# High and low weight parts of the first mixer: sixteen tiles by rounding and adding transfers instead of ScalarE and VectorE, and a moved product

## Chip, cores and metric

The kernel runs on one core of a Trainium2 chip. The metric is the device time of one execution in microseconds (us). The three runs of the kernel before lie between 2079.13 and 2080.56 us, with a median of 2079.3 us. The engines are PE (TensorE; PEld is its weight load), DVE (VectorE), ACT (ScalarE), POOL (GpSimd) and SP (SyncE, which issues transfers).

## What is computed

Two layers of a diffusion backbone over 1024 latent tokens of 1024 channels, with 256 context tokens. Layer 0 mixes tokens by a bidirectional linear recurrence (RG-LRU), layer 1 by a gated short convolution; each is followed by a gated feed-forward part with a convolution. The change lies in the first mixer, cut here to its core:

```python
def rglru_coeffs(u, w_r, b_r, w_i, b_i, lam):
    ub = u.reshape(bsz, n, LRU_HEADS, LRU_BLOCK)            # 4 heads of 256 channels
    r = sigmoid(einsum('bnhi,hij->bnhj', ub, w_r) + b_r)
    i = sigmoid(einsum('bnhi,hij->bnhj', ub, w_i) + b_i)
    log_a = LRU_C * r * log_sigmoid(lam)
    return exp(log_a), sqrt(-expm1(2.0 * log_a)) * (i * u)

def rglru_mixer(hl, hc, ...):                               # hl latent, hc context
    ul = seq_conv(hl @ w_x, conv_w, conv_b, CONV_A_PAD)
    uc = seq_conv(hc @ w_x, conv_w, conv_b, CONV_A_PAD)
    hl_f = scan of the latent, forward, from the last state of the context
    hl_b = the same, backward
    return (gelu(hl @ w_gate) * (hl_f + hl_b)) @ w_out
```

All inputs and the output are float32.

## The kernel before, in words

**Products in two parts.** A float32 operand is split into a high part, rounded to the matmul type fp32r, and a low part, the rest. A product of two split operands takes three matmuls, high by high, high by low and low by high (`mm`). The split of a weight tile (`split`, called in `weight_item`) is an ACT instruction that writes `wh` from the loaded tile `raw`, and a DVE subtraction that writes `wl` from `raw` and `wh`. Channels lie on the 128 partitions in eight chunks, tokens along the free dimension.

**Units and slots.** The program is a list of units, each with the weight tiles that it needs. The first mixer's list is the string `ORDER`:

- `g`*m* is the gate product of channel chunk *m* and `x`*m* the latent product with `w_x`: 48 matmuls of 512 columns each, one 128x1024 weight tile (`wg`, `wx`);
- `ctx` holds the eight context products xc0 to xc7, 24 matmuls of 256 columns each;
- `us`*m* splits the convolved inputs of chunks *m* and *m*+1 into `uh` and `ul`;
- `r`*m* is a recurrence block: 48 matmuls of 512 columns and 24 of 256 with two `wri` tiles, one for each direction, then tanh, exp, sqrt on ACT and products and scans on DVE in seven `mx` tiles. Both blocks of a head, r0 and r1, r2 and r3 and so on, use the same two `wri` tiles;
- `e`*n* and `d`*n* are *n* dot products of DVE over `ada` rows, which later layers need. Those of `e` go through `mx` tiles, those of `d` through the single tile `acct`.

Weight tiles live in six half-width slots, which hold three tiles of 1024 columns at a time. A slot is free when its last matmul has read it. `raw` tiles come on SP's queue into three buffers, ahead of the split. The small `cs` tile holds, before the recurrence, a weighted sum of weight rows and the squares of the context's norm; `xc` is the context itself.

**Order.** Instructions are recorded, and a planner (`Plan.flush`) sets the order on each engine by costs (`cost`), delays between engines (`lag`) and due times. PE's order is the program's own. Each engine works strictly in its order, and so does each queue of transfers. The out-projection `o` follows r7; its first unit multiplies three weight tiles with all eight output chunks of the mixer, chunk by chunk.

Of the kernel before, what the change touches and what calls it, by code (L numbers as in the profile page):

```python
# [8 lines left out]
F32 = mybir.dt.float32  # L9
F32R = mybir.dt.float32r  # L10
AF = mybir.ActivationFunctionType
ALU = mybir.AluOpType
# [5 lines left out]
HALF = 512  # L18
# [12 lines left out]
for _n, _w in _VEC:  # L31
# [10 lines left out]
DOTS = (0, 0, 0, 1, 1, 2, 2, 2)  # L42


ORDER = ("g2 shift g3 norm g4 g5 ctx mx us0 e6 x4 r0 d3 x5 d2 r1 d2 us2 x6 d1 r2 d1 x7 d1 r3 d1 us4 d1 r4 d1 g6 r5 "
         "us6 g7 r6 r7")

TABLE = {AF.Silu: (AF.Silu, AF.Tanh), AF.Gelu_apprx_tanh: (AF.Gelu_apprx_tanh, AF.Tanh), AF.Sqrt: (AF.Sqrt,),
# [3 lines left out]
class Plan:  # L52
# [48 lines left out]
    @staticmethod  # L101
    def cost(engine, op, a, k):

        if engine == "sync":
            return 4 * int(np.prod(a[0].shape)) / 360e3
        n = max(int(np.prod(v.shape[1:])) for v in list(a) + list(k.values()) if isinstance(v, bass.AP))
        if engine == "tensor":
            n = a[2].shape[-1]
            return max(n, 128) / 2400 * (4 if a[2].dtype == F32 else 1)
        if engine == "scalar":  # L110
            return 0.09 + n * 0.85e-3 + (0.09 if "accum_out" in k else 0)
        if engine == "gpsimd":
            return 0.15 + n * (2.1e-3 if op == "tensor_tensor" else 0.84e-3)
        return 0.07 + n * (6.25e-3 if op == "reciprocal" else 1.05e-3)

    @staticmethod
    def lag(a, b):

        return 0.0 if a == b else 0.95 if a == "sync" else 1.9 if b == "sync" else 0.2

    def flush(self):
        ops, first, last = self.ops, self.todo, len(self.ops)
# [61 lines left out]
def hybrid_kernel(ctx: ExitStack, tc: tile.TileContext, out, xs, cs, c, cc, ada, vecs,  # L184
                  ident, w0, wx, wg, wo, wri, wbi, wbo, wup, wdn):
    nc = Plan(tc)
    V, S, T, G = nc.vector, nc.scalar, nc.tensor, nc.gpsimd
# [37 lines left out]
    def sub(o, a, b, eng=None):  # L225
        (eng or V).tensor_tensor(out=o, in0=a, in1=b, op=ALU.subtract)

    def act(o, i, f, bias=0.0, scale=1.0):
        S.activation(o, i, f, bias=bias, scale=scale)

    def split(hi, lo, src, eng=None):
        if eng is None:
            act(hi, src, AF.Identity)
        else:
            eng.tensor_scalar(out=hi, in0=src, scalar1=1.0, scalar2=0.0, op0=ALU.mult, op1=ALU.add)
        sub(lo, src, hi.bitcast(F32))
# [17 lines left out]
    x = xp.tile([P, KD, SEQ], F32, tag="x", name="x")  # L254
# [21 lines left out]
    weight_hi = [None]  # L276
# [23 lines left out]
    def wsrc(key):  # L300
        kind = key[0]
        if kind in ("x", "xc"):
            return wx[key[1]]
        if kind == "g":
            return wg[key[1]]
        if kind == "o":
            return wo[key[1]]
        if kind == "ri":
            return wri[key[1]]
        if kind == "bo":  # L310
            return wbo[key[1]]
        return wdn[key[1], key[2], :, 2 * D:]
# [9 lines left out]
    def flat(t, i, n):  # L322
        return t[:, i:i + n].rearrange("p a b -> p (a b)") if n > 1 else t[:, i]

    def weight_item(key):
        src = wsrc(key)
        n = src.shape[-1]

        def prep(sl, raws):
            hi, lo = flat(sl[0][0], sl[0][2], len(sl))[:, :n], flat(sl[0][1], sl[0][2], len(sl))[:, :n]  # L330
            split(hi, lo, raws[0].tile[:, :n], weight_hi[0])
            return hi, lo
        return Item(key, [Raw(src)], -(-n // HALF), prep)

    def block_items(name, src1, src2, again):

# [32 lines left out]
    def run_units(nside):  # L369
# [3 lines left out]
        for i, (_, keys) in enumerate(units):  # L373
            for k in keys:
                if k not in seen:
                    seen[k] = i
                    stream.append(items[k] if k in items else weight_item(k))
                    for _ in range(nside(k)):
                        if side:
                            src, dst, bt, eng = side.pop(0)  # L380
                            stream.append(Item(None, [Raw(src)], 0, lambda sl, raws, dst=dst, bt=bt, eng=eng:
                                               dot(dst, raws[0].tile, bt, eng)))
                last[k] = i
# [487 lines left out]
    shifts = start()  # L871
    for o in ORDER.split():
        if o[0] == "g":
# [571 lines left out]
```

## Time and profile before

| What | Value |
|---|---|
| median of 3 runs | 2079.3 us |
| the profiled execution, its own time | 2082.59 us |
| its span, first to last instruction | 2080.8 us |
| PE busy | 2036.8 us (98%) |
| DVE busy | 1764.5 us (85%) |
| ACT busy | 1049.3 us (50%) |
| POOL busy | 0.2 us |
| mean granted TensorE clock | 0.993 of full speed |

The 1.8 us by which the profiled execution's time exceeds its span lie around the first and last instruction. Shares over the whole span hide the stage of interest: the first mixer lies between 100 and 400 us. A timeline row gives the start, the duration, the engine, the program line, the operation with out<-in and the shape; brackets at its end give the idle time before it and what ended that. All instructions carry line 165, that of the planner's issue, so tiles tell them apart. Consecutive instructions of DVE and ACT overlap slightly, so what one takes on its engine is read from start to start.

### The profile page before, as it was taken

To read this page: it belongs to the slowest core of one execution; us is meant where nothing else is said; L and a number is where in the kernel's file an instruction comes from. 1 tells how busy PE (TensorE), PEld (TensorE's weight loads), DVE (VectorE), ACT (ScalarE), POOL (GpSimd) and SP (SyncE) were. 2 spreads that over 40 slices of the span, in tenths; PEclk is the share of its full clock that TensorE was granted. 3 is DMA by queue.
4 is the path that set the end of the run, shared out by engine and by line. 5 is a ranking of instruction groups with operands and counts; after the bars stand their busy time and mean duration, and the time that the engine had idled before them with its cause. 6 is when DMAs were issued, how large, how long until landed. Compare 5 with 4: busy or idle time off the path is not lost.

```text
span 2080.8 us, 25029 instructions
## 1 busy us (share of the span) xinstructions
PE 2036.8 (98%) x9218; PEld 1681.5 (81%) x9218; DVE 1764.5 (85%) x2624; ACT 1049.3 (50%) x1574; POOL 0.2 (0%) x4
## 2 busy tenths in 40 slices
PE   8899989999999999999999999999999999999998
PEld 6688877787888888878888788888888888878888
DVE  7998999979888888798769988858988887688867
ACT  6366878546544444535255433435644444464345
POOL 0000000000000000000000000000000000000000
PEclk9999999999999999999999999999999999999999
DMA  7544222551334455565361345652243443474345
GB/s 298 185 169 162 71 81 84 193 167 48 126 132 157 156 174 173 174 199 162 95 194 66 114 164 197 231 192 75 83 136 128 142 137 108 137 236 142 111 140 164
DMA packets 103418, 307.05 MB, mean 148 GB/s; under 512 B 10368, under 2 KB 14720, under 8 KB 103168
## 3 DMA queue, kind: packets, MB, share of 16 engines
q1 hardware_dynamic: 103296, 305.46, 44.6%
q8 instruction: 72, 1.18, 0.2%
q14 instruction: 50, 0.41, 0.1%
HBM read 248.80 MB, written 56.62 MB: 147 GB/s over the span
## 4 chain that ended last, share of the span: by engine, by line
PE 84%; DVE 9%; ACT 4%; DMA 2%; issue 1%; SPq 0%; DVEq 0%; ACTq 0%
PE banks L165 84%; ACT mx L165 2%; DVE x L165 2%; DVE mx L165 2%; DVE u L165 2%; DVE bl L165 2%; DMA x<-in_xs 1%; DVE wl L165 1%; DMA s<-bd 1%; ACT L165 1%; ACT bh L165 1%; DMA raw<-in_wg 0%; DVE uc L165 0%; DVE ul L165 0%; DVE acct L165 0%
## 5 line engine op out<-in xcount | busy, mean ns | idle before, releaser
L165 PE MATMUL banks<-bl,wh 128*128 128x512 f32 (+1 forms) x2720 | 1052.2, 387 | 11.0 <-DVE bl L165 10.9
L165 PE MATMUL banks<-bh,wh 128*128 128x512 f32 (+1 forms) x2720 | 1054.3, 388 | 3.2 <-ACT wh L165 1.6
L165 PE MATMUL banks<-bh,wl 128*128 128x512 f32 (+1 forms) x2720 | 1051.0, 386 | 2.6 <-DVE wl L165 2.5
L165 PEld LDWEIGHTS banks<-bl,wh 128*128 128x128 f32 x2720 | 511.6, 188 | 124.7 <-DVE bl L165 21.6
L165 PEld LDWEIGHTS banks<-bh,wh 128*128 128x128 f32 x2720 | 511.8, 188 | 109.0 <-ACT wh L165 2.0
L165 PEld LDWEIGHTS banks<-bh,wl 128*128 128x128 f32 x2720 | 511.6, 188 | 108.1 <-DVE wl L165 7.3
L165 ACT ACTIVATE wh<-raw 128x512 fp32r<-128x512 f32 (+2 forms) x386 | 275.6, 717 | 475.0 <-PE banks L165 394.7
L165 DVE TENSOR_TENSOR wl<-raw,wh 128x512 fp32r<-128x512 f32 (+2 forms) x386 | 303.2, 794 | 60.4 <-ACT wh L165 56.9
L165 DVE SCALAR_TENSOR_TENSOR x<-banks,mod,x 128x512 f32<-128x512 f32 (+1 forms) x184 | 132.6, 726 | 93.3 <-PE banks L165 92.3
L165 ACT ACTIVATE s<-banks 128x512 f32<-128x512 f32 x174 | 103.8, 596 | 195.0 <-PE banks L165 191.8
L165 ACT ACTIVATE wh<-s 128x512 fp32r<-128x512 f32 x216 | 135.5, 628 | 110.4 <-DVE s L165 63.7
L165 DVE TENSOR_TENSOR wl<-s,wh 128x512 fp32r<-128x512 f32 x216 | 148.5, 688 | 38.6 <-ACT wh L165 34.9
L165 DVE TENSOR_TENSOR s<-s,banks 128x512 f32<-128x512 f32 x158 | 107.8, 683 | 37.4 <-PE banks L165 36.9
L165 DVE SCALAR_TENSOR_TENSOR x<-s,vec,x 128x504 f32<-128x504 f32 x132 | 96.4, 740 | 10.2 <-ACT x L165 9.0
L165 DVE SCALAR_TENSOR_TENSOR acct<-acct,cb 128x1024 f32<-128x1024 f32 x69 | 84.1, 1218 | 4.5 <-DMA acct<-in_ada 4.5
L165 PE MATMUL banks<-uh,wh 128*128 128x512 f32 (+1 forms) x192 | 70.8, 369 | 8.1 <-ACT mx L165 7.0
L165 PE MATMUL banks<-ul,wh 128*128 128x512 f32 (+1 forms) x192 | 70.5, 367 | 3.1 <-DVE ul L165 3.1
L165 PE MATMUL banks<-uh,wl 128*128 128x512 f32 (+1 forms) x192 | 70.2, 366 | 0.0
L165 ACT ACTIVATE bh<-s 128x512 fp32r<-128x512 f32 x88 | 51.5, 624 | 35.3 <-DMA s<-bd 34.0
L165 ACT ACTIVATE bh<-x,cols 128x512 fp32r<-128x512 f32 x64 | 45.1, 721 | 42.1 <-DVE cols L165 27.3
L165 DVE TENSOR_TENSOR x<-x,s 128x512 f32<-128x512 f32 x90 | 61.0, 686 | 0.8
L165 DVE TENSOR_TENSOR bl<-s,bh 128x512 fp32r<-128x512 f32 x88 | 57.2, 684 | 5.0 <-ACT bh L165 5.0
(154 smaller groups left out, 1702.0 us busy)
## 6 DMA issues: line engine op xcount, KB each, us to landing
raw<-in_wup SPq DMA_DIRECT2D x92, 512.0 KB, 3.6
acct<-in_ada SPq DMA_DIRECT2D x69, 512.0 KB, 3.5
bd<-x SPq DMA_DIRECT2D x48, 512.0 KB, 3.2
s<-bd SPq DMA_DIRECT2D x44, 512.0 KB, 4.5
raw<-in_wdn SPq DMA_DIRECT2D x32, 512.0 KB, 4.4
raw<-in_wdn SPq DMA_DIRECT2D x40, 384.0 KB, 3.4
raw<-in_wbi SPq DMA_DIRECT2D x26, 512.0 KB, 4.1
u<-in_ada SPq DMA_DIRECT2D x24, 512.0 KB, 4.6
```

Source lines behind the costliest of these rows:

```text
L165: getattr(getattr(self.tc.nc, e), op)(*a, **k)
```

## The change

For sixteen weight tiles (x4 to x7, the eight `wri` tiles, g4 to g7) three things replace load, rounding and subtraction. A POOL-issued transfer from the weight in main memory writes `wh` and rounds on the way. ACT writes `wl` as the negated `wh`. A second POOL-issued transfer reads the weight again and adds it to `wl`. These tiles no longer pass through `raw`. The other tiles are split as before. The planner's cost of a POOL instruction and its delay behind one change, and `x7` moves from between r2 and r3 to behind r3.

```diff
-ORDER = ("g2 shift g3 norm g4 g5 ctx mx us0 e6 x4 r0 d3 x5 d2 r1 d2 us2 x6 d1 r2 d1 x7 d1 r3 d1 us4 d1 r4 d1 g6 r5 "
+ORDER = ("g2 shift g3 norm g4 g5 ctx mx us0 e6 x4 r0 d3 x5 d2 r1 d2 us2 x6 d1 r2 d1 r3 d1 us4 d1 x7 d1 r4 d1 g6 r5 "
          "us6 g7 r6 r7")
@@ Plan.cost
+        if engine == "gpsimd":
+            return 1.2
...
-        if engine == "gpsimd":
-            return 0.15 + n * (2.1e-3 if op == "tensor_tensor" else 0.84e-3)
@@ Plan.lag
-        return 0.0 if a == b else 0.95 if a == "sync" else 1.9 if b == "sync" else 0.2
+        return 0.0 if a == b != "gpsimd" else 0.95 if a == "sync" else 6.0 if a == "gpsimd" else 1.9 if b == "sync" else 0.2
@@ weight_item
+        by_dma = key[0] in ("x", "ri") or key[0] == "g" and key[1] > 3
...
-            split(hi, lo, raws[0].tile[:, :n], weight_hi[0])
+            if by_dma:
+
+                G.dma_start(hi, src)
+                act(lo, hi.bitcast(F32), AF.Identity, scale=-1.0)
+                G.dma_start(lo, src, accum_op=ALU.add)
+            else:
+                split(hi, lo, raws[0].tile[:, :n], weight_hi[0])
             return hi, lo
-        return Item(key, [Raw(src)], -(-n // HALF), prep)
+        return Item(key, [] if by_dma else [Raw(src)], -(-n // HALF), prep)
```

**POOL, the queue of the new transfers.** Before, POOL issues nothing here. In the change, from the tiles of x4 to those of r2 and r3, it issues in this order (`wh` the rounding transfer, `wl` the adding one):

```order
L165 DMA wh<-in_wx 128x1024
L165 DMA wh<-in_wri 128x1024 x2
L165 DMA wl<-in_wx 128x1024
L165 DMA wl<-in_wri 128x1024 x2
L165 DMA wh<-in_wx 128x1024
L165 DMA wl<-in_wx 128x1024
L165 DMA wh<-in_wx 128x1024
L165 DMA wh<-in_wri 128x1024
L165 DMA wl<-in_wx 128x1024
L165 DMA wh<-in_wri 128x1024
L165 DMA wl<-in_wri 128x1024 x2
```

The adding transfer for x4 stands behind the rounding ones of both `wri` tiles of r0; the second of those waits for the slot of xc7. ACT's negations for x4 and the two `wri` tiles stand behind the last context convolutions. Those for x5, x6 and g7 stand between the two short tanh (256 columns) of the first direction of r0, r1 and r5, the block that PE computes while the tile is prepared.

**DVE, at the start of g3.** A piece of the difference (`raw,modc<-raw,ccb` are dot products, `u<-banks` the convolution of the latent product of chunk 3, which frees the bank that PE takes next, `cs<-cs` a sum of the context's norm, `wl` the split for g3):

```order
 L165 TENSOR_SCALAR cs_104<-u,cols 128x384
 L165 SCALAR_TENSOR_TENSOR cs_104<-u,cols,cs_104 128x384 x3
-L165 SCALAR_TENSOR_TENSOR raw,modc<-raw,ccb 128x1024 x2
+L165 SCALAR_TENSOR_TENSOR raw,modc<-raw,ccb 128x1024
+L165 TENSOR_TENSOR cs_104<-cs_104 128x256
 L165 SCALAR_TENSOR_TENSOR cs_104<-u,cols,cs_104 128x384 x4
+L165 SCALAR_TENSOR_TENSOR raw,modc<-raw,ccb 128x1024
 L165 SCALAR_TENSOR_TENSOR u<-banks,vec,u 128x1023
 L165 SCALAR_TENSOR_TENSOR u<-banks,vec,u 128x1022
-L165 SCALAR_TENSOR_TENSOR raw,modc<-raw,ccb 128x1024
 L165 SCALAR_TENSOR_TENSOR u<-banks,vec,u 128x1023
 L165 TENSOR_TENSOR wl<-raw,wh 128x1024
```

Of three dot products ahead of the last convolution step two are left, and one of them now stands between the `cs` sums and the convolution; a short sum is added.

**DVE, around x4.** A piece of the difference behind the last context convolution (`ul` are the low parts for r0, `x<-banks` the convolution of x4, `mx,mod` the six dot products of `e6`, `acct,mod` those of `d`):

```order
+L165 SCALAR_TENSOR_TENSOR mx,mod<-mx,cb 128x1024 x6
 L165 TENSOR_TENSOR ul<-u,uh 128x1024 x2
 L165 TENSOR_TENSOR ul<-uc,uh 128x256 x2
-L165 SCALAR_TENSOR_TENSOR mx,mod<-mx,cb 128x1024 x2
+L165 SCALAR_TENSOR_TENSOR acct,mod<-acct,cb 128x1024 x2
+L165 TENSOR_TENSOR mod<-mod,vec 128x8
 L165 SCALAR_TENSOR_TENSOR x<-banks,vec,x 128x1023
 L165 SCALAR_TENSOR_TENSOR x<-banks,vec,x 128x1022
 L165 SCALAR_TENSOR_TENSOR x<-banks,vec,x 128x1023
-L165 TENSOR_TENSOR wl<-raw,wh 128x1024
-L165 SCALAR_TENSOR_TENSOR mx,mod<-mx,cb 128x1024 x4
+L165 SCALAR_TENSOR_TENSOR acct,mod<-acct,cb 128x1024
```

All six dots of `e6` and two of `d` now come ahead of x4's convolution. Up to r0's first product of 1280 columns DVE does five dots of `d`, where it did one.

## Rows read from the trace of the kernel before

**Rows 1.** Busy time of each engine in four stretches of the mixer (us from the span's start); the columns are named in the first row.
```profile
core 0: us, PE busy (x) PEld busy (x) DVE busy (x) ACT busy (x) POOL busy (x), PEclk, DMA share, GB/s
160.00:205.00 45.00, 45.00 (x251) 39.40 (x250) 35.88 (x50) 27.38 (x30) 0.00 (x0) 1.00 0.48 169
205.00:300.00 95.00, 88.14 (x411) 73.43 (x410) 93.91 (x93) 73.24 (x76) 0.00 (x0) 0.95 0.22 72
300.00:381.00 81.00, 75.52 (x358) 63.07 (x357) 78.54 (x82) 75.11 (x81) 0.00 (x0) 0.98 0.33 108
```
**Rows 2.** PE's timeline: the first matmul of x4, of r0, of x5 and of the out-projection (behind r7), the long idle times between them, and two short ones behind r7.
```profile
169.83 0.40 PE L165 MATMUL banks<-bh,wh 128*128 128x512 f32 x1
...
180.74 0.39 PE L165 MATMUL banks<-uh,wh 128*128 128x512 f32 x1
...
194.51 0.40 PE L165 MATMUL banks<-bh,wh 128*128 128x512 f32 x1
...
273.91 0.79 PE L165 MATMUL banks<-ul,wh 128*128 128x512 f32 x1 [3.11 <-DVE ul L165]
...
287.60 0.79 PE L165 MATMUL banks<-uh,wh 128*128 128x512 f32 x1 [2.65 <-ACT mx L165]
...
358.25 0.51 PE L165 MATMUL banks<-uh,wh 128*128 128x512 f32 x1 [4.35 <-ACT mx L165]
...
364.13 0.40 PE L165 MATMUL banks<-bh,wh 128*128 128x512 f32 x1
...
367.27 0.50 PE L165 MATMUL banks<-bh,wl 128*128 128x512 f32 x1 [1.13 <-DVE wl L165]
...
391.06 0.50 PE L165 MATMUL banks<-bl,wh 128*128 128x512 f32 x1 [0.60 <-DVE bl L165]
...
394.06 0.50 PE L165 MATMUL banks<-bl,wh 128*128 128x512 f32 x1 [0.66 <-DVE bl L165]
```
**Rows 3.** PE's timeline where g2 ends and g3 begins; between them is a small product for the shift.
```profile
107.08 0.39 PE L165 MATMUL banks<-bh,wl 128*128 128x512 f32 x1
109.91 1.41 PE L165 MATMUL banks<-ones,cs 128*128 128x1 f32 x6 [2.44 <-DVE u L165]
111.18 0.77 PE L165 MATMUL banks<-bh,wh 128*128 128x512 f32 x1
```
**Rows 4.** The same windows view in steps of 2 us: behind the idle time of rows 3, and behind the short one at 367.27 us (the third column from the right is the granted clock).
```profile
110.00:112.00 2.00, 2.00 (x8) 1.90 (x9) 1.53 (x3) 1.36 (x5) 0.00 (x0) 0.50 0.63 231
...
116.00:118.00 2.00, 2.00 (x9) 1.64 (x8) 2.00 (x5) 2.00 (x3) 0.00 (x0) 0.92 0.77 264
...
368.00:370.00 2.00, 2.00 (x10) 1.63 (x10) 2.00 (x4) 2.00 (x5) 0.00 (x0) 1.00 0.85 245
```
**Rows 5.** DVE's timeline up to the split of g3.
```profile
98.68 1.22 DVE L165 SCALAR_TENSOR_TENSOR raw<-raw,ccb 128x1024 f32<-128x1024 f32 x1
...
100.97 2.58 DVE L165 SCALAR_TENSOR_TENSOR cs<-u,cols,cs 128x384 f32<-128x384 f32 x4
104.82 2.60 DVE L165 SCALAR_TENSOR_TENSOR u<-banks,vec,u 128x1023 f32<-128x1023 f32 x2 [1.27 <-ACT u L165]
107.34 1.22 DVE L165 SCALAR_TENSOR_TENSOR raw<-raw,ccb 128x1024 f32<-128x1024 f32 x1
...
109.67 1.22 DVE L165 TENSOR_TENSOR wl<-raw,wh 128x1024 fp32r<-128x1024 f32 x1
```
**Rows 6.** ACT's timeline around the end of xc7 and in x4 and r0.
```profile
169.91 1.06 ACT L165 ACTIVATE wh<-raw 128x1024 fp32r<-128x1024 f32 x1 [1.37 <-PE banks L165]
170.87 0.55 ACT L165 ACTIVATE uc<-banks,vec 128x256 f32<-128x256 f32 x1
...
187.81 0.84 ACT L165 ACTIVATE mx<-banks,vec 128x256 f32<-128x256 f32 x2 [0.31 <-PE banks L165]
```
**Rows 7.** Transfers that SP issues: size and median us from issue to landing.
```profile
acct<-in_ada SPq DMA_DIRECT2D x69, 512.0 KB, 3.5
...
raw<-in_wx SPq DMA_DIRECT2D x13, 512.0 KB, 4.3
...
mx<-in_ada SPq DMA_DIRECT2D x6, 512.0 KB, 7.2
```
**Rows 8.** DVE's timeline between x4 and the packed stretch, and in it.
```profile
182.18 3.92 DVE L165 SCALAR_TENSOR_TENSOR x<-banks,vec,x 128x1023 f32<-128x1023 f32 x3 [1.82 <-ACT x L165]
186.01 1.22 DVE L165 TENSOR_TENSOR wl<-raw,wh 128x1024 fp32r<-128x1024 f32 x1
...
199.70 1.50 DVE L165 SCALAR_TENSOR_TENSOR mx<-mx 128x1280 f32<-128x1280 f32 x1 [2.55 <-ACT mx L165]
203.64 1.49 DVE L165 TENSOR_TENSOR mx<-mx 128x1280 f32<-128x1280 f32 x1 [0.97 <-ACT mx L165]
...
212.72 1.22 DVE L165 TENSOR_TENSOR wl<-raw,wh 128x1024 fp32r<-128x1024 f32 x1
213.86 0.42 DVE L165 TENSOR_TENSOR uc<-uc,mx 128x256 f32<-128x256 f32 x1
```
**Rows 9.** DVE's costliest groups between 205 and 400 us: count, busy us, mean ns of one, idle time before. Of the 13 `wl<-raw,wh`, the last three belong to the out-projection.
```profile
L165 DVE TENSOR_TENSOR_SCAN mx<-mx 128x1280 f32<-128x1280 f32 x8 | 22.5, 2806 | 0.0
...
L165 DVE TENSOR_TENSOR wl<-raw,wh 128x1024 fp32r<-128x1024 f32 x13 | 15.8, 1212 | 0.2 <-ACT wh L165 0.2
L165 DVE SCALAR_TENSOR_TENSOR acct<-acct,cb 128x1024 f32<-128x1024 f32 x12 | 14.6, 1217 | 0.0
```

## Prediction

> **What bounds the kernel now.** I read the windows of the mixer first [rows 1]. From 205 to 381 us DVE is busy 172.5 of 176 us, the last 81 us with ACT at 75.1 as well, while PE leaves 12.3 us unused and its granted clock sinks to 0.95 and 0.98. So DVE sets the pace there and PE waits; before 205 us PE has no gap. PE's own timeline sizes the loss [rows 2]: a gate or latent product takes 180.74 - 169.83 = 10.91 us, a recurrence block 194.51 - 180.74 = 13.77 us. Six of the one and eight of the other lie between 169.83 (x4) and 364.13 (end of r7): 175.6 us of work in 194.3 us, so 18.7 us are lost. Most of it is three waits, of 3.11 us for DVE's low parts and of 2.65 and 4.35 us for ACT, which itself waits for an `mx` tile, and the half clock behind them. That half clock is best seen elsewhere: after 2.44 us without a matmul [rows 3] PE runs at 0.50 until about 116.3 us [rows 4], 12 matmuls 0.43 us apart instead of 0.23, 2.4 us lost. After the 1.13 us wait at 367.27 [rows 2] the clock stays at 1.00 [rows 4].
>
> I work against the profiled execution: its span is 2080.8 us, its time 2082.59, which is 3.3 us above the median of 2079.3. Differences are taken off the median. Some 0.2% (4.2 us) is about what a measurement of this kernel can tell from no change.
>
> **What is removed.** Sixteen subtractions on DVE, each 213.86 - 212.72 = 1.14 us [rows 8]. Five (g4, g5, x4, r0's two) lie where PE has no gap, and x5's [rows 8] lies where DVE afterwards waits 2.55 and 0.97 us for ACT: these six are worth nothing. Ten lie in the packed stretch, where thirteen such rows include three of the out-projection [rows 9]: 11.4 us. ACT gains nothing, since a negation of 1024 columns replaces each rounding of the same size. Sixteen loads leave SP's queue; their tiles were there in time, so no gain.
>
> **What moves.** Around x4 DVE does more dot products early: five of `d` instead of one ahead of r0's product at 203.64 us [rows 8]. Four more at 1.15 us leave the packed stretch: 4.6 us.
>
> At g3 a dot product leaves the way. Before, DVE does two dots, the `cs` sums (to 103.55), waits 1.27 us for ACT, then convolves with a third dot in between; the split follows at 109.67 [rows 5], and PE, waiting for the bank, resumes at 109.91 [rows 3]. In the new order: from 98.68, dot to 99.8, short sum to 100.2, `cs` sums to 102.8, the second dot inside ACT's wait, then three convolution steps of 1.28 us from 104.0 to 107.8. PE, done with g2 at 107.5, then waits some 0.6 us instead of 2.44 and goes on 1.9 us earlier. So short a wait should leave the clock up, as the 1.13 us one did, which returns the 2.4 us. **Term 1: -4.3 us.** If the clock falls all the same it is -1.9; if SP brings g3's tile no earlier, nothing.
>
> x7's move takes a cover from r2-r3 and puts it ahead of r4, whose two tiles need it; r3 uses r2's tiles and needs none. By itself it costs nothing as long as x7's tile, whose slot is free from the end of x6, has r2 and r3 (27 us) to arrive.
>
> **What is added.** Each tile now needs, after its slot is free, a rounding transfer, a negation, and an adding transfer. No row shows a POOL transfer. Bounds from SP's 512 KB [rows 7]: 3.5 us at the low end; for the adding one, which reads two streams, 2 x 4.3 = 8.6 us at the high end. I take 4.5 for rounding (near the 4.3 of the same tiles) and 6 for adding, the middle of the two ends.
>
> By the Trainium skill, page "DMA: Bandwidth & Descriptors", section "Anatomy of one DMA", a POOL-issued transfer takes about 2.0 us plus bytes over 436 GB/s, an estimate of 3.2 us for 512 KB; no run here shows it, SP's fastest median is 3.5, and by it the sum would be that of the quick rival below.
>
> *x4.* Its slot is free three context products early, but on ACT its negation stands behind the last context convolution, and on POOL its adding transfer stands behind the rounding one that waits for xc7. ACT now does xc7's convolution (0.55) at once, then the negation (about 1.0) [rows 6]: the adding transfer is issued 1.8 us after xc7 ends. At that moment the six `mx` loads start too, which took 7.2 us each in a crowd [rows 7]; I take that for it. PE, without a gap here before, waits 1.8 + 7.2 = 9.0 us and then loses 2.4 at half clock. **Term 2: +11.4 us.** Ends: 1.8 + 3.5 + 2.4 = 7.7 and 1.8 + 8.6 + 2.4 = 12.8.
>
> *x5, x6, g7.* The slot is free when the product before ends, and r0, r1 or r5 (13.77) covers the chain. ACT's negation stands behind a tanh that ends 188.2 - 180.74 = 7.5 us into the block [rows 2, 6], so it ends at 8.5, and the adding transfer lands at 14.5: 0.75 us late each, 2.2 in all, and 0 to 3.3 each between the ends. g6's negation stands earlier. The `wri` tiles have a product and half a block as cover, 10.91 + 6.9 = 17.8 us; 4.5 + 1.0 + 6 fit even with some queueing.
>
> **The sum.** If PE's own work were all: -4.3 + 11.4 - 18.7 + 2.2 = -9.4 us. But DVE must keep up. Up to 203.64 us its work is fed by PE and ACT and shifts with them (-4.3 + 11.4 + 0.75); from there it is 11.4 + 4.6 = 16.0 us shorter: **-8.2 us**. This is the later of the two, and it counts, because behind r7 PE already waits at 391.06 and 394.06 for DVE's last low parts [rows 2]. ACT's work is unchanged and 93% packed from 300 us on [rows 1]; its idle 27.7 us from 205 to 381 would have to shrink by 16. In an engine that works in order not all of this succeeds: I give 2 us back. Forecast **-6.2 us**: 2079.3 - 6.2 = **2073.1 us** (span 2074.6, the profiled execution 2076.4). What hides all other edits at no cost is PE's gapless work from 111 to 169.8 us.
>
> **Rivals.**
> *Slow adding.* The added wait takes the place of the removed one. From 7.7 us per adding transfer on (8.5 + 7.7 - 13.77 = 2.4), x5, x6 and g7 come late by as much as the wait that dropped the clock [rows 3], and I charge each the half clock too. At 8.6: -4.3 + 12.8 - 18.7 + 3 x (3.3 + 2.4) = +6.9, **2086.2 us**, slower. For it: two streams into one tile, and all sixteen tiles lose the `raw` prefetch. Against: SP's transfers of 512 KB take 3.5 to 4.5 us, and the DMA share of 0.22 to 0.33 [rows 1] leaves room. A second way there: a transfer held back by a running DVE instruction; one scan of 2.8 us [rows 9] makes 8.8 of my 6. The skill's page "SBUF — State Buffer", section "Who interferes with whom", has a VectorE instruction with two inputs contend only with GpSimd work that reads SBUF, and only the two-port modes keep such a transfer's descriptors from being written; no row here shows either. Chance 0.20, 0.04 of it for the second way.
> *ACT takes over.* If ACT, not DVE, holds r4 to r7, only half of the 18.7 returns: -4.3 + 11.4 + 2.2 - 9.4 = -0.1, **2079.2 us**. For it: ACT's 75.1 of 81 us. Against: most of its waits in there are for DVE's `mx`. Chance 0.21.
> *Quick transfers.* At 3.5 us x4 costs 7.7 and nothing else is late: -4.3 + 7.7 - 16.0 = -12.6, **2066.7 us**. Chance 0.14.
>
> **How the numbers follow.** The forecast has 0.45; 0.05 of it lies above -4.2 us. Faster by over 0.2%: 0.40 + 0.14 = 0.54. Within: 0.21 + 0.05 = 0.26. Slower: 0.20. The range takes in the quick case and the slow one at its upper bound: 2065 to 2087 us, with slower adding still left out above.
>
> **What would show it.** Right: DVE's `wl<-raw,wh` of 1024 columns fall by 16; PE's idle time ahead of g3 is under 1.2 us with no half clock behind it; one wait of 8 to 11 us ahead of x4 with half clock behind it; the waits at r4 and ahead of r7 mostly gone; waits under 1.5 us ahead of x5, x6 and g7. Wrong: adding transfers of 8 us and more with PE waiting for `wl` at each product; or ACT busy without a break from r4 on and PE's three waits still there; or longer DVE instructions beside POOL's transfers.

## The result, and the profile after

The changed kernel takes **2103.2 us** (median of 5 runs, 2099.57 to 2105.0) against 2079.3 before: ratio 1.0113, 95% interval 1.0098 to 1.0127, some 24 us **slower**. The forecast was 2073.1 with a range of 2065 to 2087, so direction and range were both missed.

The profiled execution after took 2103.19 us, span 2101.3; that of before had a span of 2080.8. Five times from PE's timelines cut both spans into stages: the first context product, the first matmul of r0, the first of the out-projection, the first norm matmul of the feed-forward part (`banks<-ones,acct`), the end.

| Stage, us | before | after | difference |
|---|---|---|---|
| up to the context products | 146.79 | 144.39 | -2.4 |
| context products, x4 | 33.95 | 48.48 | +14.5 |
| r0 to r7 with their products | 183.39 | 188.90 | +5.5 |
| out-projection | 69.78 | 71.84 | +2.1 |
| the rest | 1646.9 | 1647.7 | +0.8 |
| span | 2080.8 | 2101.3 | +20.5 |

The medians lie 23.9 us apart, not 20.5, because the profiled execution of before was 3.3 us above its median. The loss is in the first mixer alone. First the windows view of r0 to r7, as in [rows 1], before:
```profile
core 0: us, PE busy (x) PEld busy (x) DVE busy (x) ACT busy (x) POOL busy (x), PEclk, DMA share, GB/s
180.74:364.13 183.39, 172.18 (x818) 144.37 (x816) 174.00 (x176) 150.43 (x153) 0.00 (x0) 0.96 0.24 81
```
and after:
```profile
192.87:381.77 188.90, 174.02 (x818) 145.14 (x816) 156.90 (x156) 149.51 (x152) 15.71 (x22) 0.95 0.38 98
```
DVE has 17.1 us less to do, about what the prediction counted, and ACT as much as before. Yet the stretch is longer: DVE's unused time grew from 9.4 to 32.0 us. Four waits for loads of `acct` make up 14.1 us of that; before, these dot products waited for no load ([rows 9] has 0.0 us). DVE's groups between 180 and 382 us:
```profile
L165 DVE SCALAR_TENSOR_TENSOR acct<-acct,cb 128x1024 f32<-128x1024 f32 x13 | 15.9, 1220 | 14.1 <-DMA acct<-in_ada 14.1
```
PE's timeline after, answering to [rows 2, 3], shows where PE waits (brackets: idle time before the row, and what ended it):
```profile
108.90 0.80 PE L165 MATMUL banks<-ones,cs 128*128 128x1 f32 x6 [2.53 <-DVE u L165]
...
167.49 0.47 PE L165 MATMUL banks<-bh,wh 128*128 128x512 f32 x1
...
179.87 0.80 PE L165 MATMUL banks<-bh,wl 128*128 128x512 f32 x1 [11.68 <-DMA wl<-in_wx]
...
192.87 0.39 PE L165 MATMUL banks<-uh,wh 128*128 128x512 f32 x1
...
203.55 0.77 PE L165 MATMUL banks<-uh,wh 128*128 128x512 f32 x1 [3.65 <-issue]
...
213.09 0.40 PE L165 MATMUL banks<-bh,wh 128*128 128x512 f32 x1
...
278.14 0.80 PE L165 MATMUL banks<-uh,wh 128*128 128x512 f32 x1 [3.82 <-ACT mx L165]
...
368.47 0.50 PE L165 MATMUL banks<-uh,wh 128*128 128x512 f32 x1 [1.96 <-ACT mx L165]
...
377.48 0.50 PE L165 MATMUL banks<-uh,wh 128*128 128x512 f32 x1 [1.67 <-ACT mx L165]
...
381.77 0.40 PE L165 MATMUL banks<-bh,wh 128*128 128x512 f32 x1
...
386.85 0.79 PE L165 MATMUL banks<-bh,wl 128*128 128x512 f32 x1 [3.07 <-DVE wl L165]
```
The hole at x4 is 11.68 us. r0 takes 213.09 - 192.87 = 20.2 us where a block needs 13.77. From r0's end on, the blocks and products lose as much as before, at other places. DVE's timeline, answering to [rows 5, 8], explains the long r0:
```profile
101.63 1.93 DVE L165 SCALAR_TENSOR_TENSOR cs<-u,cols,cs 128x384 f32<-128x384 f32 x3 [1.95 <-DMA u<-in_w]
...
174.07 1.23 DVE L165 SCALAR_TENSOR_TENSOR mx<-mx,cb 128x1024 f32<-128x1024 f32 x1 [4.33 <-DMA mx<-in_ada]
...
180.11 1.23 DVE L165 SCALAR_TENSOR_TENSOR mx<-mx,cb 128x1024 f32<-128x1024 f32 x1 [3.00 <-DMA mx<-in_ada]
...
190.81 1.22 DVE L165 TENSOR_TENSOR ul<-u,uh 128x1024 fp32r<-128x1024 f32 x1
...
198.18 1.23 DVE L165 SCALAR_TENSOR_TENSOR acct<-acct,cb 128x1024 f32<-128x1024 f32 x1 [4.34 <-DMA acct<-in_ada]
...
199.53 3.91 DVE L165 SCALAR_TENSOR_TENSOR x<-banks,vec,x 128x1023 f32<-128x1023 f32 x3
203.37 1.22 DVE L165 SCALAR_TENSOR_TENSOR acct<-acct,cb 128x1024 f32<-128x1024 f32 x1
```
A dot product ahead of x4's convolution waits 4.34 us for a load that is not there. The convolution ends at 203.44, and at 203.55 PE goes on with r0's second direction, 0.11 us later. I read this as the bank that the convolution frees; so PE's wait named "issue" is a wait for DVE, behind a wait for a transfer. DVE does x4's convolution 17.4 us later than before (182.18 in [rows 8]), PE runs r0 12.1 us later. The new transfers, with SP's of [rows 7] (size and median us from issue to landing):
```profile
acct<-in_ada SPq DMA_DIRECT2D x69, 512.0 KB, 3.5
wh<-in_wri POOLq DMA_DIRECT2D x8, 512.0 KB, 4.5
wl<-in_wri POOLq DMA_DIRECT2D x8, 512.0 KB, 8.4
mx<-in_ada SPq DMA_DIRECT2D x6, 512.0 KB, 13.2
...
wh<-in_wx POOLq DMA_DIRECT2D x4, 512.0 KB, 4.1
wl<-in_wx POOLq DMA_DIRECT2D x4, 512.0 KB, 5.7
```
Rounding transfers take 4.1 to 5.8 us, adding ones 5.7 to 8.4 in the median (`in_wg`: 5.8 each); 4.5 and 6 had been taken. The Trainium skill's page "DMA: Bandwidth & Descriptors", section "Anatomy of one DMA", would have 3.2 us for 512 KB, an estimate from its two figures; the measurement decides.

### The profile page after: what moved, and what is told of

It reads as the page before. It is cut to its first block, busy times and chain, and to the rows that moved or that the text cites. A ratio compares the mean times of both kernels' runs of the same rounds, so it can differ in the third digit from the quotient of the medians.

```text
span 2101.3 us, 25054 instructions
## 1 busy us (share of the span) xinstructions
PE 2040.0 (97%) x9218; PEld 1683.2 (80%) x9218; DVE 1748.4 (83%) x2608; ACT 1049.1 (50%) x1574; POOL 23.2 (1%) x36
## 4 chain that ended last, share of the span: by engine, by line
PE 79%; DVE 9%; issue 7%; DMA 2%; ACT 2%; POOL 1%; SPq 0%; DVEq 0%; POOLq 0%; ACTq 0%
PE banks L165 79%; DVE bl L165 2%; DVE x L165 2%; DVE mx L165 2%; DVE u L165 1%; ACT mx L165 1%; DMA s<-bd 1%; DVE wl L165 1%; DMA acct<-in_ada 1%; ACT bh L165 0%; POOL wl L165 0%; DVE ul L165 0%; DMA x<-in_xs 0%; DVE acct L165 0%; DMA wh<-in_wg 0%
## 5 line engine op out<-in xcount | busy, mean ns | idle before, releaser
L165 PEld LDWEIGHTS banks<-bh,wl 128*128 128x128 f32 x2720 | 512.8, 189 | 123.7 <-DMA wl<-in_wx 12.1
L165 ACT ACTIVATE wh<-raw 128x512 fp32r<-128x512 f32 (+2 forms) x370 | 258.8, 702 | 467.9 <-PE banks L165 386.2
L165 DVE TENSOR_TENSOR wl<-raw,wh 128x512 fp32r<-128x512 f32 (+2 forms) x370 | 283.9, 776 | 59.6 <-ACT wh L165 56.4
L165 PE MATMUL banks<-uh,wh 128*128 128x512 f32 (+1 forms) x192 | 71.6, 373 | 13.2 <-ACT mx L165 8.0
```

The source lines that it names most:

```text
L165: getattr(getattr(self.tc.nc, e), op)(*a, **k)
```

## The experiments

All stages are cut as above, from the profiled execution of each kernel; median and ratio are of its timed runs beside the kernel before on the same chip. Profiled executions of kernels with the same instructions up to the context differ by up to 4.7 us in the first stage, so totals go by medians and only places by stages.

| Run | median | ratio, 95% interval | to ctx | ctx, x4 | r0-r7 | out-proj. | rest |
|---|---|---|---|---|---|---|---|
| before | 2079.3 | | 146.8 | 33.9 | 183.4 | 69.8 | 1646.9 |
| change | 2103.2 | 1.0113 (1.0098-1.0127) | 144.4 | 48.5 | 188.9 | 71.8 | 1647.7 |
| e1 | 2083.7 | 1.0019 (1.0010-1.0027) | 146.9 | 33.9 | 184.1 | 70.5 | 1648.4 |
| e2 | 2106.2 | 1.0133 (1.0120-1.0147) | 143.4 | 47.9 | 194.7 | 69.6 | 1647.8 |
| e3 | 2087.4 | 1.0040 (1.0028-1.0053) | 146.5 | 33.9 | 186.9 | 70.2 | 1648.2 |
| e4 | 2096.5 | 1.0084 (1.0070-1.0098) | 143.1 | 48.8 | 180.4 | 70.0 | 1650.4 |
| e5 | 2084.9 | 1.0029 (1.0018-1.0041) | 146.8 | 33.9 | 179.9 | 73.1 | 1653.1 |
| e6 | 2097.5 | 1.0089 (1.0074-1.0105) | 134.5 | 60.5 | 177.7 | 72.9 | 1650.1 |
| e7 | 2087.4 | 1.0037 (1.0024-1.0049) | 134.5 | 40.0 | 189.8 | 69.6 | 1651.3 |
| e8 | 2082.8 | 1.0015 (1.0007-1.0024) | 133.5 | 40.6 | 190.5 | 70.0 | 1646.4 |
| e9 | 2081.6 | 1.0006 (0.9997-1.0014) | 147.7 | 33.9 | 179.9 | 72.8 | 1647.7 |
| e10 | 2094.1 | 1.0059 (1.0045-1.0072) | 143.5 | 33.9 | 193.2 | 73.0 | 1646.8 |
| e11 | 2083.8 | 1.0017 (1.0008-1.0025) | 145.4 | 33.9 | 182.4 | 70.4 | 1647.5 |
| e12 | 2086.3 | 1.0030 (1.0017-1.0042) | 132.2 | 51.7 | 179.1 | 73.2 | 1648.2 |
| e13 | 2076.3 | 0.9982 (0.9973-0.9991) | 144.2 | 33.9 | 179.8 | 69.7 | 1646.8 |
| e14 | 2079.7 | 0.9993 (0.9984-1.0002) | 146.4 | 33.9 | 179.0 | 70.0 | 1647.8 |
| e15 | 2078.8 | 0.9992 (0.9983-1.0000) | 146.8 | 33.9 | 179.5 | 70.5 | 1647.3 |
| e16 | 2094.4 | 1.0064 (1.0051-1.0077) | 144.5 | 48.3 | 181.3 | 70.0 | 1648.2 |
| e17 | 2079.1 | 0.9994 (0.9985-1.0002) | 143.0 | 33.9 | 174.4 | 74.7 | 1647.5 |
| e18 | 2079.4 | 0.9999 (0.9990-1.0007) | 144.2 | 33.9 | 179.4 | 73.5 | 1646.8 |

In e6, e7, e8 and e12 g5's 10.9 us stand in a later stage than elsewhere.

### x7's move: e1 and e2
```diff
 # e1: the kernel before with
-"x6 d1 r2 d1 x7 d1 r3 d1 us4 d1 r4"
+"x6 d1 r2 d1 r3 d1 us4 d1 x7 d1 r4"
 # e2: the change with that line turned round
```


> The kernel before with only x7 moved behind r3; all tiles split as before. Theory A (the move costs by itself: in the changed kernel r3, which now follows r2 without a product between, takes 20.6 us instead of 13.77, and the two waits that r4 had before, 3.11 and 2.65 us, do not pay for it): 2 to 7 us slower, 2081 to 2086 us. Theory B (the move only shifts waits about, as the prediction said): within 2 us of 2079.3.

> The changed kernel with x7 back between r2 and r3. Theory A (the move costs): r3's 3.82 us wait goes, 2097 to 2101 us. Theory B (the move is free; the loss is the hole at x4, 12.1 us, and r0, 6.4 us too long): the same as the change, 2103 +- 2 us, with the hole at x4 still 11 to 12 us and DVE idle again some 15 us longer than before between r0's first long product and the end of r7.

By itself the move costs some 4 us (2 to 6 by the interval), inside the change it seems worth some 3 (2103.2 against 2106.2, with overlapping intervals, so this is not shown). Both are small beside 24 us: the move shifts the pair of blocks that has no product between (r3 and r4 before, r2 and r3 after). Neither theory had both signs. Where e1's 4 us arise is open: its stages differ by at most 1.5 us each from those before.

### The hole and the dots: e3, e4, e16, e5, e9
```diff
 # e3: weight_item of the change
-by_dma = key[0] in ("x", "ri") or ...
+by_dma = key not in (("x", 4), ("ri", 0), ("ri", 1)) and (key[0] in ("x", "ri") or ...)
 # e4: Plan.flush of the change; late() stands in for self.lag() at its three places
+slow = {"mx": 8.0, "acct": 3.0}
+late = lambda p, i: self.lag(...) + (slow.get(<name of p's output>, 0.0) if ops[p][0] == "sync" else 0.0)
 # e5: e3 and e4 together
 # e16 and e9: e4 and e5 with slow = {} from the third flush on (behind the first mixer)
```


> The changed kernel, but x4 and the two wri tiles of r0 are loaded and split as before; the other 13 tiles by transfers, x7 behind r3. DVE's order around x4 is that of the kernel before again. Theory A (the hole at x4 and the early dot products that follow from it are the loss; past them the shorter DVE work changes nothing, since the chain of ACT and DVE between PE's blocks sets the pace): 2103.2 - 12.1 - 6.4 = 2084.7, or down to 2079. Theory B (DVE's shorter work counts once the hole is gone, as the prediction had it): -2.3 at g3 and -8 to -12 in the packed stretch, 2065 to 2070 us. Theory C (transfers slow the packed stretch whatever stands ahead): above 2088 us.

> The changed kernel with one difference in the planner: it adds 8 us to the delay behind a load of an mx tile and 3 us behind one of acct, so that dot products are placed later (the first ul of r0 comes ahead of the six mx dots, and one acct dot instead of two ahead of x4's convolution). The work and the transfers are the same. Theory A (the early dots lengthen r0 by 6.4 us): r0 takes 14 to 15 us and the time falls to 2095 to 2099 us; if the 7.2 us that DVE waits for acct in r5 and r6 also count, to 2090 to 2095. Theory B (the dots only fill time that DVE would have waited for ACT anyway): 2103 +- 2 us.

> The whole change with the planner's longer delay behind loads for dot products in the first mixer only. From e4, whose mixer ended 11.3 us earlier than the change's and whose feed-forward part was 2.7 us longer: 2103.2 - 11.3 = 2092 us if the two add up (range 2090 to 2095); 2096 us if e4's longer feed-forward part was chance.

e4 came out by theory A, with a feed-forward part 2.7 us longer, a side effect of the delay there; e16 confines the delay. In e16 the work and the transfers are the change's, only the planned order differs, DVE's above all. r0 on PE's timeline of e16, its first matmul and that of x5:
```profile
192.82 0.39 PE L165 MATMUL banks<-uh,wh 128*128 128x512 f32 x1
...
206.59 0.40 PE L165 MATMUL banks<-bh,wh 128*128 128x512 f32 x1
```
13.77 us again, from 20.2. By medians the **early dots cost 2103.2 - 2094.4 = 8.8 us** (10 by the ratios, whose intervals do not overlap). In e3 (2087.4 us, between theories A and C) the hole is gone, but the dots still wait 9.4 us for `acct` elsewhere, and a 4.95 us wait of PE for `ul` follows.

> Both mends together: x4 and the two wri tiles of r0 split as before, and the planner's longer delay behind loads for dot products. Theory A (the early dots and the hole at x4 were all that went wrong; what is left are waits of blocks that follow a block directly): e3's 9.4 us of DVE waits for acct and the 4.95 us wait of PE for ul go, 2079 to 2083 us, with waits of 3 to 4 us for ACT still in r3 and in r7. Theory B (DVE's total sets the pace, so that 12 us less on it count): 2068 to 2073 us. Theory C (the dots only changed places): 2087 us as e3.

> e5 with the planner's longer delay behind loads for dot products confined to the first mixer (in e5 it also held in the feed-forward part, which became 6 us longer: from the first norm matmul behind the mixer to the end 1653.1 us against 1646.9 before). Theory A: the feed-forward part returns to 1647 to 1648 us, and the whole comes to 2079 to 2081 us, even with the kernel before although DVE has some 12 us less to do in the mixer. Theory B (the 6 us come from the mixer's tail): 2084 to 2086 us as e5.

e5's 2084.9 us lie outside all three theories. By its stages the same side effect is 6 us there (the profiled execution was its slowest; the medians of e5 and e9 differ by 3.3 us); e9 is without it. From e16 to e9 the **three tiles behind the context cost 2094.4 - 2081.6 = 12.8 us** (12 by the ratios); the stages put 14.4 us at x4 and 1.3 of it back into r0 to r7. With both mended e9 cannot be told from the kernel before. That settles the loss, and leaves a question: DVE has 11.0 us less to do in r0 to r7 than before, and in the total nothing comes of it. The windows view of that stage in e9, and PE's timeline:
```profile
181.60:361.52 179.92, 169.83 (x818) 142.16 (x817) 162.99 (x167) 149.07 (x152) 15.74 (x22) 0.98 0.42 110
```
```profile
262.65 0.50 PE L165 MATMUL banks<-uh,wh 128*128 128x512 f32 x1 [3.80 <-ACT mx L165]
...
357.23 0.50 PE L165 MATMUL banks<-uh,wh 128*128 128x512 f32 x1 [3.09 <-ACT mx L165]
...
367.05 0.79 PE L165 MATMUL banks<-bh,wl 128*128 128x512 f32 x1 [3.52 <-DVE wl L165]
```
The waits stand in the second blocks of pairs (r3, r7), and a third one is in the out-projection: r0 to r7 are 3.5 us shorter, the out-projection 3.1 longer.

### Cover for the chain: e6 and e12
```diff
 # e6: e4 with
-"norm g4 g5 ctx mx us0 e6 x4"
+"norm g4 ctx g5 mx us0 e6 x4"
 # e12: e16 with the same line, and g5 by load and split:  key[0] == "g" and key[1] > 3 and key[1] != 5
```


> e4 (the whole change with the dot products placed later) with g5 moved from ahead of the context products to between them and x4, so that x4's two transfers have 10.9 us of PE work as cover. Theory A (the hole is the chain of the adding transfer behind the freed slot, 11 to 12 us long, and cover pays for it): the hole at x4 shrinks from 10.6 to under 3 us, no half clock there, and as the context products may now start up to 4 us late: 2083 to 2089 us against e4's 2096.5. Theory B (the transfer is late because the engines' queues hold it until the first products end, whatever stands between): the hole stays above 8 us, 2094 us and more.

> The whole change with the longer delay in the mixer only, and g5, loaded and split as before, between the context products and x4 (in e6 g5 itself went by transfers, so that the hole of 11.25 us only moved to g5). Theory A (the hole is a chain of some 11 us behind the slot that the context products free, and 10.9 us of PE work cover it): PE waits under 2 us for x4's low part, mixer's first norm matmul at 433 to 438 us, 2081 to 2086 us. Theory B (the low part stays late): a wait of 8 us and more at x4, 2090 us and more.

e6 failed as a test: g5 goes by transfers itself, and the hole of 11.25 us moved to g5. e12 mends that; PE's timeline of e12 at x4:
```profile
171.77 0.50 PE L165 MATMUL banks<-bh,wl 128*128 128x512 f32 x1 [1.95 <-DMA wl<-in_wx]
```
So 11.6 us (e16) become 1.95 with one product as cover, and the time falls by 8.1 us. The adding transfer itself took as long as in the change (10.15 and 10.28 us), so the hole is this chain behind a slot that comes free, without cover. e12 stays 4.7 us above e9.

### Filling the pair: e7 and e8
```diff
 # e7: e5 with g5 from behind g4 to between r2 and r3:  "r2 d1 g5 r3"
 # e8: the kernel before with g5 from behind g4 to:  "us4 d1 g5 r4"
```


> e5 with g5 moved between r2 and r3. Theory A (a block right behind a block waits for ACT, because one block keeps ACT busy for longer than PE's 13.77 us; a product between pays for it): r3 takes 13.8 to 14.5 us, without its wait of 3.8 us and the half clock behind, 4 to 7 us off e5; the context products may start up to 4 us late. 2074 to 2080 us. Theory B (DVE's or ACT's total over the stretch sets the pace): the wait comes back somewhere else, the same as e5 or up to 4 us slower.

> The kernel before (all tiles split on ACT and DVE) with g5 moved between r3 and r4, its only pair without a product between besides r6 and r7. Theory A (pairs of blocks wait for ACT): the waits of 3.11 and 2.65 us around r4 go, with the half clock behind them 6 to 8 us; the context products may start up to 4 us late: 2073 to 2078 us. Theory B (DVE's total sets the pace there, as the prediction took it): DVE's work is unchanged, so the waits go to r5 to r7 and the time stays at 2079 to 2083 us.

Both came out by theory B: the wait of the filled pair went, but 4.32 us (e8) and 2.85 us (e7) ahead of x4 came, and x7's tile (1.95 us in e7) and r3 (2.44 us for DVE's convolution in e8) waited instead. The new waits stand where g5 used to give cover, so neither run speaks for DVE's total, theory B's reason in e8. g5, the one product tried, was not spare.

### What sets the waits: e10, e11, e13, e14, e15
```diff
 # e10: e9 with
-act(lo, hi.bitcast(F32), AF.Identity, scale=-1.0)
+G.tensor_scalar(out=lo, in0=hi.bitcast(F32), scalar1=-1.0, scalar2=0.0, op0=ALU.mult, op1=ALU.add)
 # (the planner takes 1.6 us for it, and a delay of 0.2 us behind it)
 # e11: the kernel before, 13 tiles as in e3, raw still loaded:
+G.dma_start(hi, src)
+sub(lo, raws[0].tile[:, :n], hi.bitcast(F32))
 # e13: the kernel before, dots of d:  dot(dst, t[:, :24], bt[:, :24], eng)
 # e14: e9, negation:  act(lo[:, :24], hi[:, :24].bitcast(F32), AF.Identity, scale=-1.0)
 # e15: e9 with both; in e13 to e15 cost() counts 24 columns as 1024, so the order stays
```


> e9 with the negation of each of the 13 tiles on POOL instead of ACT (ACT loses 13 instructions of about 1 us). Theory A (once DVE is relieved, ACT sets the pace where two recurrence blocks follow each other and at the mixer's end: 351 to 369 us without a break in e4): 3 to 8 us off e9, the waits for ACT in r3 and r7 shorter by 1 to 2 us each. Theory B (neither engine's total but the chain of dependent steps of a block sets the waits): within 2 us of e9. Theory C (POOL's instruction is slow, or DVE is slower beside it): the low parts come later and x5, x6, g6, g7 wait, slower than e9 by 3 us and more.

e10 is slower, but not by theory C alone: the planner put r1's scans ahead of x6's convolution, and PE's wait of 4.68 us at 244.91, again named "issue", ends where that convolution ends (DVE's timeline of e10):
```profile
237.93 3.07 DVE L165 TENSOR_TENSOR_SCAN mx<-mx,u 128x1024 f32<-128x1024 f32 x1
240.92 3.89 DVE L165 SCALAR_TENSOR_TENSOR u<-banks,vec,u 128x1023 f32<-128x1023 f32 x3
```
Theory C shows as well: in r0 to r7 DVE is busy for 173.4 us, where e9 had 163.0 in its own, and a dot product that begins beside a negation takes 2.06 us instead of 1.22 (last section). So e10 says nothing clean on ACT.

> The kernel before with only the rounding by transfer for the 13 tiles behind r0's (g4 to g7 among them): raw is still loaded by SP and DVE still subtracts, ACT loses 13 roundings of 1.06 us, and no adding transfer is there. ACT alone is relieved, x7 stands at its old place. Theory A (DVE, idle for 1.9 us between 204 and 365 us, sets the pace of the kernel before): no gain, 2078 to 2082 us. Theory B (ACT sets the waits at pairs of blocks): 3 to 6 us faster, 2073 to 2076 us.

ACT has 10.4 us less to do in r0 to r7, and the time is not shorter; why it is some 4 us longer by medians, outside both theories, stays open, as its profiled execution (2081.5 us) was its shortest.

> The kernel before with the 13 dot products of d in the mixer taken over 24 columns instead of 1024 (that part of the sums is left out); loads, order and everything else unchanged, since the planner is given the old cost. DVE has 14 us less to do, 12 of them between 204 and 365 us. Theory A (the prediction's: DVE's total sets the pace there): 8 to 12 us faster, 2067 to 2071 us. Theory B (waits at blocks behind blocks hang on the chain PE, ACT, DVE, ACT and not on DVE's total): 0 to 3 us faster, 2076 to 2080 us, and DVE's idle time rises from 1.9 to over 10 us, as it did in the change.

> e9 with the 13 negations taken over 24 columns instead of 1024 (the low parts lack that term); order, transfers and waits between engines unchanged, since the planner is given the old cost. ACT has about 12 us less to do. Theory A (with DVE relieved, ACT's total sets the pace): 4 to 9 us off e9, 2073 to 2078 us. Theory B (the chain sets the waits): within 2 us of e9, as its waits in r3 and r7 have no negation in front of them.

> e9 with both short negations and short dot products of d (both parts left out as in e13 and e14). DVE then has some 26 us and ACT 12 us less to do than in the kernel before. Theory A (totals): the waits in r3 and r7 and those at the out-projection all but vanish, 2063 to 2070 us. Theory B (the chain of a block): the waits for ACT in r3 (3.8 us) and in r7 (3.1 us) remain within 1 us of their size, 2075 to 2081 us.

The windows view of r0 to r7 in e13:
```profile
178.15:357.94 179.79, 171.13 (x818) 143.31 (x816) 161.63 (x176) 150.16 (x153) 0.00 (x0) 0.97 0.23 84
```
and in e15:
```profile
180.75:360.26 179.51, 170.61 (x818) 143.22 (x816) 151.59 (x169) 140.64 (x152) 15.74 (x22) 0.97 0.43 114
```
At an unchanged order, 12.4 us less on DVE make e13's blocks 3.6 us shorter and its time 3.4 us (1.9 to 5.6), not the 8 to 12 of theory A. e15 takes another 11.4 us of DVE and 8.4 us of ACT out of e9: its blocks gain 0.4 us. The wait in r7 is 3.17 us, where e9 had 3.09, that in r3 2.48 (3.80 in e9). The short negations alone (e14) leave 3.18 and 2.47, and theory B's 2 us around e9 hold (2079.7). They do take 2.8 us off the out-projection, whose wait falls from 3.52 to 1.96. So no engine's total sets the wait in r7, and that in r3 shrinks by a third.

### What stands in front of the wait: e17 and e18
ACT's timeline of e9 ahead of PE's wait in r7 (the last row is the tanh that frees the bank for 357.23):
```profile
348.04 2.96 ACT L165 ACTIVATE mx<-mx,sp 128x1280 f32<-128x1280 f32 x2
351.02 1.28 ACT L165 ACT_TABLE_LOAD   x1
352.31 2.43 ACT L165 ACTIVATE mx<-mx 128x1280 f32<-128x1280 f32 x2
354.76 1.28 ACT L165 ACT_TABLE_LOAD   x1
356.06 1.11 ACT L165 ACTIVATE mx<-banks,vec 128x1024 f32<-128x1024 f32 x1
```
A table load, the two square roots of r6, a table load back: 5.0 us in front of the tanh. No negation and no dot product is in it. The kernel before had the same piece ahead of its wait at 358.25 [rows 2], as ACT's timeline of before shows, with no idle time in it:
```profile
352.04 1.28 ACT L165 ACT_TABLE_LOAD   x1
353.34 2.43 ACT L165 ACTIVATE mx<-mx 128x1280 f32<-128x1280 f32 x2
355.79 1.28 ACT L165 ACT_TABLE_LOAD   x1
357.08 1.11 ACT L165 ACTIVATE mx<-banks,vec 128x1024 f32<-128x1024 f32 x1
```
```diff
 # ri(), and the emission in Plan.flush; pairs: m in (2, 6) on e9 (e17), m in (3, 6) on the kernel before (e18)
 act(Tn, Tn, AF.Sqrt, scale=0.25)
+m in (2, 6) and nc.copies.add(len(nc.ops) - 1)
+a = (a[0], a[1], AF.Identity) if i in self.copies else a
```


> e9 with the square roots of r2 and r6, the first blocks of its two pairs, replaced by copies of the same size (the square root is left out there), order unchanged; so ACT needs no table load ahead of them and none behind: two loads of 1.28 us fewer in each pair. Theory A (ACT's piece of table load, two square roots, table load ahead of the tanh that frees PE's bank sets the wait): the wait in r3 falls from 3.80 to some 1.2 us and that in r7 from 3.09 to some 0.5 us, and what the half clock took behind them (0 to 2 us each) is saved too: 5 to 8 us off e9, 2074 to 2077 us. Theory B (the wait is for an mx tile that DVE frees, so that ACT would only wait earlier): the waits stay within 1 us of their size, 2080 to 2082 us.

> The kernel before with the square roots of r3 and r6 (the first blocks of its two pairs) replaced by copies in the same way, order unchanged, DVE's and ACT's other work unchanged. Theory A (the table loads): the wait of 2.65 us in r4 falls to under 0.5 us, that of 4.35 us in r7 to some 1.8 us; the 3.11 us wait for DVE's low part of us4 stays: 4 to 7 us faster, 2072 to 2075 us. Theory B (DVE, packed, or the mx tiles set it): 2078 to 2080 us.

PE's timeline of e17 at the same three places:
```profile
253.52 0.50 PE L165 MATMUL banks<-uh,wh 128*128 128x512 f32 x1 [0.97 <-ACT mx L165]
...
347.05 0.50 PE L165 MATMUL banks<-uh,wh 128*128 128x512 f32 x1 [0.32 <-ACT mx L165]
...
358.62 0.80 PE L165 MATMUL banks<-bh,wl 128*128 128x512 f32 x1 [3.95 <-DVE wl L165]
```
Both waits fall by 2.8 us, as theory A had it, and r0 to r7 by 5.5. In e18 the waits are 0 (was 2.65) and 2.60 (was 4.35) us. But the totals do not follow: e17 is only 2.4 us off e9, outside both theories, and e18 cannot be told from the kernel before, as theory B had it. Of what the blocks gain, the out-projection gives back 1.8 us more than in e9 (e17) and 3.7 us (e18). Its wait is an order on DVE, to be read in the change's own timeline ahead of 386.85:
```profile
382.05 2.35 DVE L165 TENSOR_TENSOR_SCAN mx<-mx,u 128x1024 f32<-128x1024 f32 x1
384.44 1.23 DVE L165 TENSOR_TENSOR mx<-mx 128x1024 f32<-128x1024 f32 x1
385.58 1.22 DVE L165 TENSOR_TENSOR wl<-raw,wh 128x1024 fp32r<-128x1024 f32 x1
```
The low part that PE wants at once stands behind r7's last scan. Moving it ahead of the scan was not tried. No version beat the kernel before in a computation left whole.

## Why the prediction was wrong

**The step that failed: DVE's work is "11.4 + 4.6 = 16.0 us shorter", and this sum "counts".** I took the later of two sums, that of PE's own waits and that of DVE's work, and DVE's decided. The sizes were right (17.1 us less by the windows). The conclusion was not: from r0's end to the end of r7 the change gains 183.39 + 6.4 - 188.90 = 0.9 us; e16, without the waits for `acct`, gains 2.1 there, and e9 3.5. That DVE was busy 98% of a stretch did not make its total the limit: e13 took 12.4 us of work out at the same order and got 3.4. What ends the waits is the piece of ACT's order with two table loads (e17: 5.5 us), and what then comes is DVE's order at the out-projection. I had read that ACT "itself waits for an `mx` tile" ahead of the waits of 2.65 and 4.35 us. In the trace of before ACT works without a break from 276.22 us to the tanh that ends the first, and from 346.44 us to the one that ends the second. I had "ACT takes over" as a rival, but as ACT's total, which does not set the wait in r7 either (e14, e15).

**The second failure: early dots as a gain of 4.6 us.** The front part shows them ahead of x4's convolution, and I counted what they take off later, not what they wait for and who waits behind them. Their loads take 3.5 us (`acct`, one buffer) and 7.2 to 13.2 (`mx`), while the planner reckons with some 2.4 (512 KB over 360 GB/s, and 0.95). With a planned gap of PE at x4 it filled DVE with them. Cost: 8.8 us (e16). In place of the gain of 4.6, r0 alone became 6.4 us longer.

**Term 2, right in kind, too small.** A hole with half clock behind it: 14.5 us, not 11.4. The adding transfer, issued at 169.55, let PE go on at 179.87, so 10.3 us and not 7.2. Those for x5, x6 and x7 took 5.5, 5.9 and 5.4 us; beside x4's the six `mx` loads ran, from 7.2 to 13.2 themselves, and two adding ones for `wri`, and I put the difference down to them (no run took them apart). e12 shows that the hole is this chain. The price of the three tiles by medians is 12.8 us (e9, e16).

**Term 1 did not come about.** The context products come 2.4 us earlier, not 4.3, but not by this: the wait at g3 stayed (2.53 us) with half clock behind it, g2 had ended 1.1 us earlier, and profiled executions differ by up to 4.7 us in this stage. DVE's `cs` sums wait 1.95 us for a load of `u` at 101.63, and ACT starts the convolution at 103.59, as before (103.58). I had shortened DVE's list and not asked for its inputs.

**Right:** x5, x6 and g7 wait 0, 0 and 0.37 us for their transfers (0.75 each forecast); 16 subtractions less; ACT's work unchanged; DVE's dot product takes 1.23 us beside POOL's transfers as without them. Both ways of the rival with slow adding fell: what it needed, x5, x6 and g7 late, did not come, and two adding transfers issued while a scan ran (at 232.89 and 259.86 us) landed after 5.93 and 5.44 us. **Wrong besides:** x7's move, "by itself it costs nothing", was 4 us (e1); and SP's fastest median at 512 KB is 3.2 us (`bd<-x`), not 3.5, which touches no term.

Put together against the 20.5 us of the spans: -2.4 (g3), +14.5 (x4), +6.4 (r0), -0.9 (r1 to r7), +2.1 (out-projection), +0.8 (rest). Against the -8.2 of the DVE sum, the largest miss is 15.1 us, the 16.0 that brought 0.9; next come r0's 6.4 and x4's 3.1.

## What to carry to other kernels

A packed engine is not yet the bound: look at the five instructions in front of the one that ends each wait, and count a saving only where it is one of them; taking the work out at an unchanged order measures that in one run. Where a change opens a gap in one engine's plan, read what the planner puts there and when its inputs land. A chain of two dependent transfers and an instruction behind a freed buffer took some 11 us here and needed a whole product (10.9 us) as cover; without one, the three tiles behind the gap were better left to the old way (e9).

## What the runs showed of the hardware

**Similar waits, different clocks.** Ahead of g3 PE waited 2.44 us before, and the granted clock was 0.50 behind it, the 1.2 GHz level [rows 3, 4]. In e10 it waited 2.48 us at the same place and the clock stayed full (PE's timeline, then the windows view):
```profile
109.63 0.80 PE L165 MATMUL banks<-ones,cs 128*128 128x1 f32 x6 [2.48 <-DVE u L165]
```
```profile
112.00:116.00 4.00, 4.00 (x19) 3.34 (x18) 3.76 (x7) 3.94 (x6) 1.95 (x2) 1.00 0.54 138
```
The idle time alone did not tell whether the clock falls. Such a wait cost its length, or with half clock some 2 us more: 2.4 before, and an estimated 1.7 in the change, from ten matmuls behind its 2.53 us wait that start 0.40 us apart in the mean instead of 0.23.

**POOL's arithmetic beside DVE.** A scan of 1024 columns that began while POOL's negation ran in e10 took 3.07 us; the mean of these scans is 2.34 in e9 and in the change, beside POOL's transfers. A dot product that began so took 2.06 us instead of 1.22 (e10, POOL's and DVE's timelines):
```profile
184.40 1.58 POOL L165 TENSOR_SCALAR wl<-wh 128x1024 fp32r<-128x1024 f32 x1 [6.16 <-DMA wh<-in_wx]
```
```profile
185.00 2.06 DVE L165 SCALAR_TENSOR_TENSOR mx<-mx,cb 128x1024 f32<-128x1024 f32 x1
```
A convolution around the negation at 284.99 us, with a bank of PE among its inputs, kept its 3.92 us. By the Trainium skill, page "SBUF — State Buffer", section "Who interferes with whom", a VectorE instruction with two SBUF inputs contends with GpSimd work that reads SBUF; these rows agree.

**A table switch** on ACT, start to start, cost 1.29 or 1.30 us in each of the rows above.
